# Another order of the second MLP product, projection operands ahead of the last norms, and loads a step apart, in a two-layer decoder trunk

## The chip, the cores and the metric

One core of one Trainium2 chip runs the kernel. The metric is device time in microseconds (us). Names of engines are those of the profile: PE is TensorE's matmuls, PEld its weight loads, DVE is VectorE, ACT is ScalarE, POOL is GpSimd, SP is SyncE, which issues most DMAs.

## What is computed

`x` is 1024 rows of 1024 float32 numbers. Two layers run one after the other: layer 0 mixes rows with causal pooling, layer 1 with a gated DeltaNet. Behind each mixer stand a norm, a dense MLP with a gated embedding, and a second norm.

```python
for i in range(2):
    mix = pool_mixer(x, ...) if i == 0 else gated_deltanet(x, ...)
    x = layer_norm(ALPHA * x + mix, ln_gain[i, 0], ln_bias[i, 0])
    ff = square(relu(x @ w1[i])) @ w2[i]              # 1024 -> 4096 -> 1024
    pe = sigmoid(x @ gate_w[i] + gate_b[i]) * (p[i] @ ple_proj[i])
    x = layer_norm(ALPHA * x + ff + pe, ln_gain[i, 1], ln_bias[i, 1])
```

The DeltaNet projects `x` onto queries, keys, values, a gate `z` and two narrow columns (`x @ w_in`), convolves over rows, runs a recurrence over eight chunks of 128 rows whose state `St` passes from chunk to chunk, norms each chunk's output, and multiplies by `w_out`.

## The kernel before

**Arithmetic.** Nearly every float32 product is three matmuls: each operand is split into a high part (a cast on ACT, L68) and a remainder (a subtraction on DVE, L69), and `mm3` (L71) adds high x high, high x low and low x high. So what PE can start on is mostly decided by when ACT and DVE have split an operand, and before that by when the DMA into a `raw` tile has landed. There are three `raw` slots (L40), two slots each for the `wh` and `wl` split results (L39) and six `tmp` slots.

**Order of work.** The program is written in one order, and a scheduler at build time settles the order on each engine from it by priorities; each engine then runs its list in that order. Where an instruction waits, all behind it on the same engine wait.

**Layer 0, start** (`layer0`, L567): `pp` is a list of 16 units that multiply `p` by `ple_proj` and store the result (`embed_unit`, L173: six matmuls, an ACT copy, a DMA issued from ACT). Four of them run first (L601), the others by a tuple of counts per step (L655).

**Gate and first product.** `gate` (L234) ends with operands for a seven-product (Winograd) scheme of the MLP's two products; the last, `t3`, is cut from `ra` at L303. In `mlp` (L306), `prep_a` (L332) makes operands of `w1` and `multiply_a` (L366) uses them, three steps behind.

**Second product** (L478 to L551): seven products P1, P2, P5, P6, P7, P4, P3 of eight groups `g` each. A group is 24 matmuls of 128x512 (four row tiles `tt`, two halves, three matmuls); `prep_b` prepares one group ahead. Rows of tiles 0 to 3 are finished when P4 ends, tiles 4 to 7 when P3 ends. In P3 the norms of tiles 0 to 3 run at `g` = 1 to 4. `finish` (L676) stores a row tile and transposes it for the projection (`transpose_split`, L128). In layer 0 the calls are held back by a list with a lag of four, so that tiles 0 to 3 are transposed among the last norms, and tiles 4 to 7 in the first units of the projection. The last two groups of P3 are done tile by tile (L549), each tile with its norm behind it. I call these 48 matmuls the tail; layer 1 has 96 of them.

**Projection** (`project`, L691): units of 16 or 24 matmuls; the first are `ba` half 0 (L928 loads it), `K` 0 half 0, `K` 1 half 0, `ba` half 1. Their `w_in` tiles are loaded one unit ahead.

**Recurrence** (`chain`, L970; loop at L1130): for each chunk `n` the products on the state, the output, `turn(n - 1)` (ACT scales the output at L1104, PE transposes it at L1109) and the per-chunk norm. At the end of chunk 5 the code loads all four pieces of the first half of `w_out` (L1157). `mix_out` (L1170) multiplies by it and serves as filler in chunk 7.

Of the kernel before, what the change touches and what calls it, by code (L numbers as in the profile page):

```python
# [32 lines left out]
def trunk(ctx: ExitStack, tc: tile.TileContext, io: dict):  # L33
# [43 lines left out]
    def load_wsm(src):  # L77
        raw = new_raw()
        nc.sync.dma_start(raw, src)
        wh = wsm.tile([P, 8, P], F32R, tag="wh", name=nm("wh"))  # L80
        wl = wsm.tile([P, 8, P], F32R, tag="wl", name=nm("wl"))
        split(wh, wl, raw.rearrange("p (k c) -> p k c", k=8))
        return wh, wl

# [67 lines left out]

    def load_w_half(wk, src, nh):
        for kk in range(4):
            raw = new_raw().rearrange("p (k c) -> p k c", k=2)
            nc.sync.dma_start(
                raw, src[kk * 256:(kk + 1) * 256, nh * 512:(nh + 1) * 512].rearrange("(k p) c -> p k c", p=P))
            split(wk[0][:, 2 * kk:2 * kk + 2, :], wk[1][:, 2 * kk:2 * kk + 2, :], raw)
# [75 lines left out]
    def gate(i, x, acc, wk, gb, early, pending):  # L234
# [68 lines left out]
        cut(t3, ra)  # L303
        return (b11h, b11l), (b21h, b21l), t2, t1, t3, t4, (b22h, b22l)

    def mlp(i, r1, acc, row, finish=None, lag=0, out=None):  # L306
# [18 lines left out]
        with tc.tile_pool(name=f"mlp{i}", bufs=5) as q:  # L325
# [180 lines left out]
            left = []  # L506

            def norm(t):
                layer_norm(acc(t), stats(t), g2, b2, True, None if out is None else out[t * P:(t + 1) * P, :])
                if finish:  # L510
                    left.append(lambda t=t: finish(t))
                if len(left) > lag:
                    left.pop(0)()

            seq = [(k, g) for k in (P1, P2, P5, P6, P7, P4, P3) for g in range(8)]
# [4 lines left out]
            for n in range(3):  # L520
                prep_a(*order[n])
            for n, o in enumerate(order):
# [8 lines left out]
            for n, (k, g) in enumerate(seq):  # L531
                if n % 2 == 0 and 4 + n // 2 < 16:
                    load_w2(4 + n // 2)
                if (k, g) == (P3, 0):
# [17 lines left out]
        return left  # L552
# [14 lines left out]
    def layer0(pool):  # L567
# [33 lines left out]
        for f in pp[0:4]:  # L601
            f()
        del pload[0:2], pp[0:4]
# [5 lines left out]
        for step in range(11):  # L609
# [45 lines left out]
            for _ in range((0, 2, 4, 2, 2, 2, 0)[min(step, 6)]):  # L655
# [14 lines left out]
        return gate(0, x1, acc, wk, gb, early, []), acc  # L670

    with tc.tile_pool(name="l0", bufs=4) as pool:
        r1, acc = layer0(pool)
# [6 lines left out]
    left = mlp(0, r1, acc, 1, finish, 4)  # L680
# [10 lines left out]
    def project(gd, pool, x2, left, heads, g, ex, ahead):  # L691
# [234 lines left out]
        w = {}  # L926

        def load_ba():  # L928
            raw = new_raw().rearrange("p (k c) -> p k c", k=8)
            nc.sync.dma_start(raw.rearrange("p k c -> p (k c)"), io["w_in"][32])  # L930
            wb = [h4(new_tmp(F32R, "wb")) for _ in range(2)]
            for z, w4 in enumerate(wb):
                r = raw[:, 4 * z:4 * z + 4, :]
                A.copy(w4[:, :, 0:64], r[:, :, 0:64])
                V.tensor_tensor(w4[:, :, 64:128], r[:, :, 64:128], w4[:, :, 0:64].bitcast(F32), ALU.subtract)
            return wb, None
# [33 lines left out]
    def chain(gd, heads, g, ex):  # L970
# [154 lines left out]
        def run(pool, stats):  # L1125
# [3 lines left out]
            pp = embed1(pool)  # L1129
            for n in range(8):  # L1130
# [8 lines left out]
                both(solve, n)  # L1139
                both(kq, n + 1)  # L1140
# [5 lines left out]
                both(output, n)  # L1146
                both(turn, n - 1)
# [4 lines left out]
                if n == 6:  # L1152
                    for t in range(8):
                        nc.sync.dma_start(acc(t), x2_d[t * P:(t + 1) * P, :])
                if n == 5:
                    wk = new_wk()
                    load_w_half(wk, io["w_out"], 0)  # L1157
                    acc = new_acc()
                    fill = [lambda t=t: mix_out(oT, wk, acc, stats, t, 0) for t in range(8)]
            for k, f in enumerate(fill):  # L1160
                if k == 2:
# [22 lines left out]
    with tc.tile_pool(name="gd", bufs=1) as gd:  # L1184
# [3 lines left out]
        with tc.tile_pool(name="gdp", bufs=1) as pool:  # L1188
            project(gd, pool, x2, left, heads, g, ex, [(64, load0), (65, prepare)])
# [4 lines left out]
    with tc.tile_pool(name="l1", bufs=4) as pool:  # L1194
# [12 lines left out]
        r1 = gate(1, x3, acc, wk, gb, [], left)  # L1207
    mlp(1, r1, acc, 3, out=io["out"])
# [62 lines left out]
```

## Time and profile before

| | us |
|---|---|
| median of 3 runs | 2176.24 (2175.05 to 2176.48) |
| the profiled execution | 2175.76 |
| its span | 2174.0 |
| PE busy | 2128.4 (98%) |
| DVE busy | 1527.0 (70%) |
| ACT busy | 1065.9 (49%) |

PE is busy nearly throughout, so the idle stretches of PE, one by one, are what can be read for time: a row of the timeline gives the start of a group of instructions, its length, engine, line, operation, and in brackets how long the engine was idle before it and what ended the wait. The granted clock is 1.00 at 2.4 GHz and 0.50 at 1.2 GHz.

### The profile page before, as it was taken

The numbers are of one execution on the slowest core, as the hardware profiler recorded it, in microseconds if no ns is written. First come the engines' busy times: TensorE is split into PE (matmuls) and PEld (weight loads), VectorE is DVE, ScalarE is ACT, GpSimd is POOL, SyncE is SP. The second block draws the span as 40 slices with busy tenths as digits, with TensorE's granted clock in tenths as the row PEclk, the third lists the DMA queues.
The fourth block names the chain that finished last, engine by engine and source line by source line (L and its number), as shares of the span: only waits on it lengthen the run. The fifth ranks groups of instructions, "written<-read, shape, count | busy, mean of one in ns | idle before, by whom it ended". The sixth has DMA issues, their size and how long they took to land.

```text
span 2174.0 us, 27706 instructions
## 1 busy us (share of the span) xinstructions
PE 2128.4 (98%) x10322; PEld 1780.0 (82%) x10322; DVE 1527.0 (70%) x2569; ACT 1065.9 (49%) x1822; POOL 25.2 (1%) x85
## 2 busy tenths in 40 slices
PE   7999999999999989999999999999999999999998
PEld 7977888887888868888888998888788888788886
DVE  7996666667765676879976677588666666677458
ACT  6434555553333446644456666453355555433334
POOL 0000000000000000000001000000000000000000
PEclk9999999999999999999999999999999999999999
DMA  8324444469333241341233545312344445943223
GB/s 303 111 83 146 151 151 143 152 225 334 100 116 97 97 163 49 100 124 49 92 131 109 139 127 177 95 68 83 117 150 159 151 147 178 331 155 116 97 96 126
DMA packets 156700, 300.98 MB, mean 138 GB/s; under 512 B 39891, under 2 KB 53587, under 8 KB 156245
## 3 DMA queue, kind: packets, MB, share of 16 engines
q1 hardware_dynamic: 151956, 290.82, 40.4%
q10 hardware_dynamic: 4608, 8.39, 1.0%
q8 instruction: 81, 1.33, 0.3%
q14 instruction: 55, 0.44, 0.1%
HBM read 208.99 MB, written 90.18 MB: 138 GB/s over the span
## 4 chain that ended last, share of the span: by engine, by line
PE 91%; DVE 4%; DMA 2%; ACT 2%; issue 1%; SPq 0%; ACTq 0%; DVEq 0%
PE ps L75 27%; PE ps L74 27%; PE ps L73 27%; PE ps L134 1%; PE ps L801 1%; DMA raw<-in_w 1%; PE ps L775 1%; PE ps L1057 1%; PE ps L1021 1%; PE ps L1079 1%; PE ps L1045 0%; PE ps L1050 0%; PE ps L1066 0%; DMA raw<-in_gate 0%; PE ps L1014 0%
## 5 line engine op out<-in xcount | busy, mean ns | idle before, releaser
L73 PE MATMUL ps<-rh,lh 128*128 128x512 f32 x896 | 349.2, 391 | 4.3 <-ACT rh L68 3.7
L74 PE MATMUL ps<-rl,lh 128*128 128x512 f32 x896 | 349.0, 390 | 0.3 <-DVE rl L69 0.3
L75 PE MATMUL ps<-rh,ll 128*128 128x512 f32 x896 | 349.0, 390 | 0.0
L68 ACT CAST lh<-raw 128x1024 fp32r<-128x1024 f32 x112 | 118.2, 1055 | 342.3 <-PE ps L74 325.7
L69 DVE TENSOR_TENSOR rl<-w,rh 128x1024 fp32r<-128x1024 f32 x110 | 134.6, 1224 | 185.5 <-issue 165.4
L73 PE MATMUL ps<-xh,wo 128*128 128x512 f32 x512 | 200.1, 391 | 3.0 <-ACT wo L68 1.6
L73 PE MATMUL ps<-xh,wh 128*128 128x512 f32 x512 | 202.7, 396 | 0.0
L73 PEld LDWEIGHTS ps<-rh,lh 128*128 128x128 f32 x896 | 168.5, 188 | 40.6 <-ACT rh L68 4.6
L75 PE MATMUL ps<-xh,wl 128*128 128x512 f32 x512 | 200.0, 391 | 1.1 <-DVE wl L69 1.1
L75 PE MATMUL ps<-xh,wo 128*128 128x512 f32 x512 | 199.8, 390 | 0.0
L74 PE MATMUL ps<-xl,wo 128*128 128x512 f32 x512 | 199.7, 390 | 0.0
L74 PE MATMUL ps<-xl,wh 128*128 128x512 f32 x512 | 199.4, 389 | 0.0
L74 PEld LDWEIGHTS ps<-rl,lh 128*128 128x128 f32 x896 | 168.6, 188 | 35.9 <-DVE rl L69 1.0
L75 PEld LDWEIGHTS ps<-rh,ll 128*128 128x128 f32 x896 | 168.5, 188 | 35.0 <-DVE ll L69 0.3
L69 DVE TENSOR_TENSOR wo<-raw,wo 128x512 fp32r<-128x512 f32 x192 | 132.1, 688 | 52.2 <-ACT wo L68 52.2
L68 ACT CAST wo<-raw 128x512 fp32r<-128x512 f32 x192 | 119.3, 621 | 99.3 <-PE ps L75 70.3
L324 DVE TENSOR_TENSOR c<-ps,c 128x512 f32<-128x512 f32 x96 | 66.4, 692 | 135.1 <-PE ps L75 72.6
L73 PE MATMUL ps<-xt,wo 128*128 128x512 f32 x384 | 149.8, 390 | 2.1 <-ACT wo L68 2.1
L74 PE MATMUL ps<-xt,wo 128*128 128x512 f32 x384 | 149.6, 390 | 0.0
L75 PE MATMUL ps<-xt,wo 128*128 128x512 f32 x384 | 149.0, 389 | 0.0
L69 DVE TENSOR_TENSOR ll<-raw,lh 128x1024 fp32r<-128x1024 f32 x112 | 136.7, 1220 | 6.7 <-ACT lh L68 6.4
L68 ACT CAST rh<-w 128x1024 fp32r<-128x1024 f32 x110 | 115.1, 1049 | 5.3 <-DMA h_d<-c 2.7
(304 smaller groups left out, 4164.8 us busy)
## 6 DMA issues: line engine op xcount, KB each, us to landing
raw<-h_d SPq DMA_DIRECT2D x112, 512.0 KB, 3.3
raw<-in_w SPq DMA_DIRECT2D x64, 512.0 KB, 3.6
w<-in_w SPq DMA_DIRECT2D x32, 1024.0 KB, 6.6
h_d<-c SPq DMA_DIRECT2D x64, 512.0 KB, 2.8
raw<-in_w_in SPq DMA_DIRECT2D x41, 512.0 KB, 3.6
h_d<-hs SPq DMA_DIRECT2D x32, 512.0 KB, 3.6
pp_d<-tmp ACTq DMA_DIRECT2D x32, 256.0 KB, 3.8
raw<-in_gate SPq DMA_DIRECT2D x16, 512.0 KB, 5.3
```

Source lines behind the costliest of these rows:

```text
L68: A.copy(hi, src)
L69: V.tensor_tensor(lo, src, hi.bitcast(F32), ALU.subtract)
L73: T.matmul(ps, lh, rh, start=first, stop=False, skip_group_check=more)
L74: T.matmul(ps, lh, rl, start=False, stop=False, skip_group_check=more)
L75: T.matmul(ps, ll, rh, start=False, stop=last, skip_group_check=more)
L134: T.transpose(pss[q][:, j, :], y[:, k * P:(k + 1) * P], ident)
L324: add = lambda o, a, b: V.tensor_tensor(o, a, b, ALU.add)
L775: T.transpose(ps[:, j, :], chunk(tiles, half * 4 + j, h), ident)
L801: T.matmul(ps[:, j, :], kc, kc, start=True, stop=True)
L1021: T.matmul(pq[:, j, :], hc("K", n, h), hc("Q", n, h), start=True, stop=True)
L1057: T.matmul(pv[:, j, :], d["X"][:, h, :], d["c"][:, 2 + gi, j], start=True, stop=True)
L1079: T.matmul(po[:, j, :], d["dt"][gi][:, j, :], d["c"][:, 4 + gi, j], start=True, stop=True)
```

## The change

1. Layer 0 starts with two `pp` units and not four; the two others run at step 0.
2. `gate` hands back the cut of `t3`, and `mlp` calls it after its first three `prep_a`.
3. The second product runs P1, P5, P6, P7, P4, P2, P3. Tiles 0 to 3 are finished after the fifth of them; their norms run in the sixth (P2) at `g` = 1, 3, 5, 7, and their `finish` in P3 at `g` = 0 to 3. The operand of P4 is made in P4 and no longer in P6, and `w2` comes in the order in which the products want it.
4. `load_ba` moves out of `project`. The operands of the first two units (`ba`, `K` 0) are loaded and split at the head of the tail, `K` 1 ahead of its last row tile; the split tiles of `K` 0 take two of the three `raw` slots, since both `wsm` slots are in use.
5. The four pieces of `w_out` are fetched at chunk 4 (end), 5 (middle), 5 (end) and 6 (start), each split one such point later (`w_step`). `turn(7)` moves one `mix_out` back.

```diff
-        cut(t3, ra)
-        return (b11h, b11l), (b21h, b21l), t2, t1, t3, t4, (b22h, b22l)
+        return [(b11h, b11l), (b21h, b21l), t2, t1, t3, t4, (b22h, b22l)], lambda: cut(t3, ra)
...
-                f, c, e, b = n // 4 % 2, n // 8, n // 2 % 2, n % 2
+                (f, c), e, b = ((0, 0), (0, 1), (1, 1), (1, 0))[n // 4], n // 2 % 2, n % 2
...
-                    sub(b21, b21, b11)
...
                 elif k == P4:
-                    r = b21
+                    sub(b11, b21, b11)
+                    r = b11
...
-            seq = [(k, g) for k in (P1, P2, P5, P6, P7, P4, P3) for g in range(8)]
+            seq = [(k, g) for k in (P1, P5, P6, P7, P4, P2, P3) for g in range(8)]
...
             for n in range(3):
                 prep_a(*order[n])
+            cut_t3()
...
-                if k == P3 and 0 < g < 4:
-                    norm(g - 1)
-                if k == P3 and g == 4:
-                    norm(3)
+                if k == P2 and g % 2:
+                    norm(g // 2)
+                if k == P3 and g < 4 and finish:
+                    finish(g)
...
+                    if last and ahead and tt in (0, 3):
+                        for f in ahead[tt]:
+                            f()
...
-        for f in pp[0:4]:
+        for f in pp[0:2]:
...
-            for _ in range((0, 2, 4, 2, 2, 2, 0)[min(step, 6)]):
+            for _ in range((2, 2, 4, 2, 2, 2, 0)[min(step, 6)]):
...
+    ahead = {0: [lambda: load_first(("ba", 0), None), lambda: load_first(("K", 0), rawp)],
+             3: [lambda: load_first(("K", 1), None)]}
...
+                kk = {(4, 2): 0, (5, 0): 1, (5, 2): 2, (6, 0): 3, (6, 1): 4}.get((n, z))
...
+                    split_w(wk, kk - 1, raw.pop(kk - 1))
+                if kk < 4:
+                    raw[kk] = fetch_w(io["w_out"], 0, kk)
...
-                    wk = new_wk()
-                    load_w_half(wk, io["w_out"], 0)
```

What the scheduler makes of it is seen at three places. The first is DVE at the head of the projection. Before, the remainders of `ba` (`wb`) stand between the steps of the last norms (L108 to L121 is one norm):

```order
L69 TENSOR_TENSOR wl_820_6127<-raw_818_6124,wh_819_6126 128x1024
L113 RECIPROCAL lnsm_206_1634<-lnsm_206_1634 128x1
L108 SCALAR_TENSOR_TENSOR acc_15_154<-acc_15_154,lnsm_206_1634,gb_745_5662 128x1024
L118 SCALAR_TENSOR_TENSOR lnsm_206_1634<-lnsm_206_1634 128x1
L109 TENSOR_SCALAR lnsm_206_1634<-lnsm_206_1634 128x1
L935 TENSOR_TENSOR wb_816_6118<-raw_815_6116,wb_816_6118 128x4x64
```

After, both `wb` and the remainder of `K` 0 (`wl_798`) stand ahead of the first take of the tail (L502):

```order
L91 TENSOR_TENSOR wb_794_5985<-raw_793_5983,wb_794_5985 128x4x64
L91 TENSOR_TENSOR wb_795_5986<-raw_793_5983,wb_795_5986 128x4x64
L69 TENSOR_TENSOR rl_792_5978<-w2_558_4378,rh_791_5977 128x1024
L69 TENSOR_TENSOR ll_790_5976<-raw_788_5973,lh_789_5975 128x1024
L69 TENSOR_TENSOR wl_798_5994<-raw_796_5991,wh_797_5993 128x1024
L502 SCALAR_TENSOR_TENSOR acc_15_154,lnsm_206_1630<-ps_539_4244,acc_15_154 128x512
```

So the operands of the first two units moved from among the last steps of the norms to ahead of all four. The second place is ACT in chunk 6. Before, two `w_out` casts (`wkh`), with their waits for DMAs, stand ahead of the eight scalings that PE's transposes wait for (L1104):

```order
L68 CAST wkh_1508_10958<-raw_1512_10968 128x1024
L1058 COPY ctr_1487_10802<-ps_1532_11052 128x512
L68 CAST wkh_1508_10958<-raw_1513_10972 128x1024
L68 CAST phl_1523_11019<-praw_1522_11018 128x256
L1008 COPY wt_1530_11044<-ps_1529_11035 64x512
L68 CAST oh_1556_11242<-oT_1354_9982 128x1024
L68 CAST oh_1561_11284<-oT_1354_9982 128x1024
L1104 ACTIVATE ctr_1448_10570<-ctr_1448_10570,f_1506_10935 128x128 x8
```

After:

```order
L1068 COPY ctr_1490_10806<-ps_1531_11046 128x512
L68 CAST oh_1556_11242<-oT_1354_9982 128x1024
L1114 ACTIVATE ctr_1448_10570<-ctr_1448_10570,f_1510_10943 128x128 x4
L68 CAST wkh_1472_10740<-raw_1532_11054 128x1024
L1114 ACTIVATE ctr_1448_10570<-ctr_1448_10570,f_1510_10943 128x128 x4
L68 CAST oh_1561_11284<-oT_1354_9982 128x1024
```

One cast and one `oh` moved out from ahead of the scalings, and the last piece of `w_out` now stands in the middle of them. The third place is ACT in the first 25 us. Before, four copies (L179) with their DMA issues (L180) stand between the two halves of `zt`, of which the last two, the second half of `zt`, `bias` and the next `wh` are:

```order
L179 COPY tmp_21_182<-ps_20_175 128x512
L179 COPY tmp_23_192<-ps_22_185 128x512
L180 DMA pp_d_78<-tmp_21_182 128x512
L180 DMA pp_d_78<-tmp_23_192 128x512
L68 CAST zt_11_131<-ps_26_211 128x512
L648 CAST bias_227<-pbr_126 128x1024
L68 CAST wh_28_233<-raw_27_231 128x1024
```

After, two of the four stand behind `wh`:

```order
L68 CAST zt_11_131<-ps_22_191 128x512
L661 CAST bias_207<-pbr_126 128x1024
L68 CAST wh_24_213<-raw_23_211 128x1024
L194 COPY tmp_28_228<-ps_27_221 128x512
L194 COPY tmp_30_238<-ps_29_231 128x512
```

## Rows read from the trace of the kernel before

**Rows 1.** The page, busy time of each engine, its share of the span, instructions

```profile
PE 2128.4 (98%) x10322; PEld 1780.0 (82%) x10322; DVE 1527.0 (70%) x2569; ACT 1065.9 (49%) x1822; POOL 25.2 (1%) x85
```

**Rows 2.** Timeline of PE, groups behind an idle stretch (idle and releaser in brackets)

```profile
22.05 0.58 PE L73 MATMUL ps<-zt,b0h 128*128 128x256 f32 x1 [2.35 <-ACT zt L68]
...
806.11 0.76 PE L953 MATMUL ps<-xh,wb 128*128 128x512 f32 x1 [9.19 <-DVE lnsm L112]
...
1337.10 1.50 PE L1109 MATMUL ps<-identr,ctr 128*128 128x128 f32 x5 [3.37 <-ACT ctr L1104]
...
1553.44 0.66 PE L73 MATMUL ps<-xt,wo 128*128 128x512 f32 x1 [1.05 <-ACT wo L68]
...
2147.75 0.50 PE L73 MATMUL ps<-rh,lh 128*128 128x512 f32 x1 [0.56 <-ACT lh L68]
```

**Rows 3.** Windows: from:to, length, busy us of PE, PEld, DVE, ACT, POOL; clock, DMA

```profile
1318.40:1323.40 5.00, 5.00 (x46) 5.00 (x46) 3.78 (x8) 4.86 (x15) 0.00 (x0) 1.00 0.59 186
21.00:28.00 7.00, 5.43 (x22) 4.85 (x23) 5.48 (x8) 3.42 (x4) 0.00 (x0) 0.51 0.85 267
...
761.00:767.00 6.00, 6.00 (x29) 4.95 (x28) 5.93 (x11) 3.81 (x6) 0.00 (x0) 1.00 0.82 310
...
799.00:810.00 11.00, 3.90 (x10) 3.16 (x11) 10.03 (x22) 5.89 (x10) 0.00 (x0) 0.53 0.57 201
1338.60:1345.40 6.80, 6.80 (x35) 5.66 (x35) 4.26 (x10) 2.57 (x9) 0.00 (x0) 0.50 0.42 159
1553.60:1557.00 3.40, 3.40 (x9) 2.61 (x10) 3.40 (x7) 1.24 (x2) 0.00 (x0) 0.50 1.02 393
```

**Rows 4.** Timeline of PE in the first projection unit, at either clock

```profile
806.67 0.63 PE L954 MATMUL ps<-xl,wb 128*128 128x512 f32 x1
...
809.23 0.53 PE L954 MATMUL ps<-xl,wb 128*128 128x512 f32 x1
809.60 0.40 PE L953 MATMUL ps<-xh,wb 128*128 128x512 f32 x1
...
811.19 0.39 PE L954 MATMUL ps<-xl,wb 128*128 128x512 f32 x1
```

**Rows 5.** Timeline of ACT in the first 25 us

```profile
19.87 1.07 ACT L179 COPY tmp<-ps 128x512 f32<-128x512 f32 x2 [0.68 <-ACT tmp L179]
...
21.41 0.59 ACT L68 CAST zt<-ps 128x512 fp32r<-128x512 f32 x1 [0.47 <-ACT tmp L179]
```

**Rows 6.** Timeline of ACT ahead of layer 1's MLP

```profile
1547.96 2.01 ACT L68 CAST xt<-ra 128x1024 fp32r<-128x1024 f32 x2 [3.73 <-PE ps L74]
```

**Rows 7.** Timelines of DVE and ACT from the tail to the projection

```profile
783.11 1.22 DVE L69 TENSOR_TENSOR ll<-raw,lh 128x1024 fp32r<-128x1024 f32 x1
...
785.63 0.68 DVE L487 SCALAR_TENSOR_TENSOR acc<-ps,acc 128x512 f32<-128x512 f32 x1
...
786.67 0.69 DVE L139 TENSOR_TENSOR xl<-ps,xh 128x512 fp32r<-128x512 f32 x1 [0.35 <-ACT xh L137]
...
788.79 1.28 DVE L108 SCALAR_TENSOR_TENSOR acc<-acc,lnsm,gb 128x1024 f32<-128x1024 f32 x1 [1.31 <-ACT junk L106]
...
806.01 0.16 DVE L113 RECIPROCAL lnsm<-lnsm 128x1 f32<-128x1 f32 x1
...
807.40 0.42 DVE L935 TENSOR_TENSOR wb<-raw,wb 128x256 fp32r<-128x256 f32 x1
...
804.02 0.69 ACT L934 CAST wb<-raw 128x256 fp32r<-128x256 f32 x2
```

**Rows 8.** Timelines of SP, ACT and DVE in chunk 6 of the recurrence

```profile
1323.77 1.76 SPq L156 DMA_DIRECT2D raw<-in_w_out  x2
...
1332.77 1.05 ACT L68 CAST wkh<-raw 128x1024 fp32r<-128x1024 f32 x1 [3.24 <-DMA raw<-in_w_out]
...
1336.65 2.45 ACT L1104 ACTIVATE ctr<-ctr,f 128x128 f32<-128x128 f32 x8
...
1333.85 1.22 DVE L69 TENSOR_TENSOR wkl<-raw,wkh 128x1024 fp32r<-128x1024 f32 x1 [3.27 <-ACT wkh L68]
```

More of the change, by code (lines that the diff above doesn't have):

```diff
@@ L75, in mm3, with load_wsm, load_ba @@
         T.matmul(ps, ll, rh, start=False, stop=last, skip_group_check=more)
-    def load_wsm(src):
+    def load_wsm(src, pool=None):
         raw = new_raw()
         nc.sync.dma_start(raw, src)
-        wh = wsm.tile([P, 8, P], F32R, tag="wh", name=nm("wh"))
-        wl = wsm.tile([P, 8, P], F32R, tag="wl", name=nm("wl"))
+        wh, wl = ((pool or wsm).tile([P, 8, P], F32R, tag="raw" if pool else s, name=nm(s)) for s in ("wh", "wl"))
         split(wh, wl, raw.rearrange("p (k c) -> p k c", k=8))
         return wh, wl
+    def load_ba():
+        raw = new_raw().rearrange("p (k c) -> p k c", k=8)
+        nc.sync.dma_start(raw.rearrange("p k c -> p (k c)"), io["w_in"][32])
+        wb = [h4(new_tmp(F32R, "wb")) for _ in range(2)]
+        for z, w4 in enumerate(wb):
+            r = raw[:, 4 * z:4 * z + 4, :]
+            A.copy(w4[:, :, 0:64], r[:, :, 0:64])
+            V.tensor_tensor(w4[:, :, 64:128], r[:, :, 64:128], w4[:, :, 0:64].bitcast(F32), ALU.subtract)
+        return wb, None
     def load_bc(pool, row):
@@ L151, in new_wk, with fetch_w, split_w @@
         return k8("wkh"), k8("wkl")
+    def fetch_w(src, nh, kk):
+        raw = new_raw().rearrange("p (k c) -> p k c", k=2)
+        nc.sync.dma_start(
+            raw, src[kk * 256:(kk + 1) * 256, nh * 512:(nh + 1) * 512].rearrange("(k p) c -> p k c", p=P))
+        return raw
+    def split_w(wk, kk, raw):
+        split(wk[0][:, 2 * kk:2 * kk + 2, :], wk[1][:, 2 * kk:2 * kk + 2, :], raw)
     def load_w_half(wk, src, nh):
         for kk in range(4):
[L155 to L158, printed above, removed]
+            split_w(wk, kk, fetch_w(src, nh, kk))
     def cols(nh):
@@ L302, in gate, with mlp @@
         t3 = new_t()
-        cut(t3, ra)
-        return (b11h, b11l), (b21h, b21l), t2, t1, t3, t4, (b22h, b22l)
-    def mlp(i, r1, acc, row, finish=None, lag=0, out=None):
+        return [(b11h, b11l), (b21h, b21l), t2, t1, t3, t4, (b22h, b22l)], lambda: cut(t3, ra)
+    def mlp(i, r1, cut_t3, acc, row, finish=None, ahead=None, out=None):
         P1, P2, P6, P5, P7, P4, P3 = range(7)
@@ L551, in mlp @@
                         norm(4 + tt)
-        return left
+        return [lambda t=t: finish(t) for t in range(4, 8)]
     x2_d = dram.tile([S, D], F32, name="x2_d")
@@ L678, in finish, with load_first @@
         transpose_split(acc(t), x2, t)
-    left = mlp(0, r1, acc, 1, finish, 4)
+    first = {}
+    def load_first(key, pool):
+        first[key] = load_ba() if key[0] == "ba" else load_wsm(io["w_in"][8 + key[1]], pool)
+    ahead = {0: [lambda: load_first(("ba", 0), None), lambda: load_first(("K", 0), rawp)],
+             3: [lambda: load_first(("K", 1), None)]}
+    left = mlp(0, r1, cut_t3, acc, 1, finish, ahead)
     def sm(pool, s, dt=F32):
@@ L689, in chunk, with project @@
         return tiles[n // 4][:, h, (n % 4) * P:(n % 4 + 1) * P]
-    def project(gd, pool, x2, left, heads, g, ex, ahead):
+    def project(gd, pool, x2, left, first, heads, g, ex, ahead):
         xh, xl = x2
@@ L925, in project @@
             at(u, f)
[L926 to L936, printed above, removed]
+        w = dict(first)
         def weights(k):
@@ L1129, in run, with w_step @@
             pp = embed1(pool)
+            wk, raw = None, {}
+            def w_step(n, z):
+                nonlocal wk
+                kk = {(4, 2): 0, (5, 0): 1, (5, 2): 2, (6, 0): 3, (6, 1): 4}.get((n, z))
+                if kk is None:
+                    return
+                if kk == 0:
+                    wk = new_wk()
+                else:
+                    split_w(wk, kk - 1, raw.pop(kk - 1))
+                if kk < 4:
+                    raw[kk] = fetch_w(io["w_out"], 0, kk)
             for n in range(8):
@@ L1188, in trunk @@
         with tc.tile_pool(name="gdp", bufs=1) as pool:
-            project(gd, pool, x2, left, heads, g, ex, [(64, load0), (65, prepare)])
+            project(gd, pool, x2, left, first, heads, g, ex, [(64, load0), (65, prepare)])
         with tc.tile_pool(name="gdc", bufs=1) as pool:
@@ L1206, in trunk @@
         load_w_half(wk, io["gate"][1], 0)
-        r1 = gate(1, x3, acc, wk, gb, [], left)
-    mlp(1, r1, acc, 3, out=io["out"])
+        r1, cut_t3 = gate(1, x3, acc, wk, gb, [], left)
+    mlp(1, r1, cut_t3, acc, 3, out=io["out"])
 def _layout(i):
```

18 lines of the change are left out of this document (8 added, 10 removed).

## The prediction

> **What bounds the kernel now.** I began with the busy times: PE works 2128.4 of 2174.0 us [rows 1]. The change removes and adds no matmul, so only PE's idle stretches and its stretches at half clock can go. The second view is PE's timeline, read for the brackets that give an idle stretch and its releaser [rows 2]: the reader is to see that the large ones are few, 9.19 us at the head of the projection, 3.37 in chunk 6 of the recurrence, 2.35 at the start, 1.05 at an MLP's start (0.79 of the same kind stand just ahead of it, and layer 0 has the same pair), 0.56 near the end. The third is the table of windows [rows 3]: the granted clock is 0.50 to 0.53 in four places, each behind or within such a stretch. What half clock costs is read in one product that runs through the change [rows 4]: six matmuls between 806.67 and 809.23 start 0.427 us apart, seven from 809.60 to 811.19 start 0.227 apart. So a matmul of 128x512 loses 0.2 us, and a stretch at half clock loses about 47% of its length. I sum against the profiled execution, 2175.76 us (span 2174.0 and 1.8 around it), which is 0.5 under the median of 2176.24.
>
> **Start of layer 0.** PE idles 2.35 us for the second half of `zt`, which ACT casts at 21.41 behind two `pp` copies from 19.87 on with their DMA issues [rows 5]. These two copies now stand behind `bias` and `wh`. The cast can come up to 21.41 - 19.87 = 1.5 us earlier. PE loses the cover of 12 matmuls there and waits for `pwt` instead, earlier; the 12 come back as fill. I take -1.5. Bounds: -3 if the half clock of 21 to 28 goes too (at most 3.3 us by the 47%), +1 if the copies, now among step 0's norm, hold it up.
>
> **Start of both MLPs.** Two casts of `t3` take 2.01 us of ACT [rows 6] ahead of an operand for which PE then idles [rows 2]. In the new order these casts still stand ahead of the operand on ACT; on DVE, though, an add and a subtraction for the next operands have moved ahead of the remainders of `t3`, and PE has products that need `t3` to run meanwhile. Of the pair of waits (1.84 us a layer) I take 1.1 away in each layer; in layer 1 also a little of the half clock of 1553.6 to 1557.0, whose 3.4 us cost 1.6 [rows 3]: -1.1 and -1.3. Bounds: 0 and 0, or -1.8 and -3.4.
>
> **Second product.** The counts of splits, subtractions, norms and loads stay; so does the pattern of accumulators (P2's first matmuls wait for takes of P4 where P5's waited for those of P2). What moves are four norms from P3 to P2, every second group, and eight transposes a group into P3. Before, both lay together: from 761 to 767 DVE was busy 5.93 of 6.00 us, and PE still 6.00 of 6.00 at full clock [rows 3]. Spread out they cost nothing; if DVE were late by a whole norm a group, that is the slow rival below. One new wait: the tail now has no transposes to fill in. The last group's left operand needs slots that the group before the tail frees, so its cast and remainder (1.22 on DVE [rows 7], about as much on ACT) lie beside only six matmuls, 6 x 0.227 = 1.4 us, though PE's list has the next tile's matmuls in between. I take +0.5 (0 to 1.1). In layer 1 the norms of tiles 0 to 3 leave the stretch ahead of the 0.56 us wait [rows 2], a wait for a load that had no `raw` slot, because each norm takes one: -0.8 with what stands beside it (0 to -0.9). The last norm and the store behind the last matmul are unchanged.
>
> **Head of the projection.** Before, PE waits from 796.9 to 806.11 for `wb`, whose cast ACT makes at 804.02 and whose second remainder DVE makes at 807.40, among the last norms [rows 7]. DVE is the busy one: 10.03 of 11.00 us from 799 to 810 [rows 3]. The change puts `wb` and `K` 0 ahead of the tail's takes. What goes is 9.19, and 8 x 0.2 = 1.7 for the half clock behind it: 10.9. What is late next? From the start of the tail, PE has 48 + 16 matmuls (tail, `ba`) = 14.5 us, then a transpose of tile 4, then 24 (`K` 0) = 5.4, so it asks for tiles 5 and 6 at about 21, then `K` 1, so for tile 7 at about 28. DVE has until then: 1.1 waiting for the last cast, two splits of 1.22, then per norm two passes of 1.28, a take of 0.68 and some seven small steps like the 0.16 one [rows 7], 4.4 in all, and between the norms of tiles 5 and 6 the remainder of `K` 1 (1.22). Three norms are done at 1.1 + 2.4 + 13.2 + 1.2 = 18, four at 23, plus waits on ACT of up to 3. So tiles 5 and 6 come just in time, tile 7 with 2 us to spare. DVE fits because the eight remainders of `finish` (0.69 each, 5.5 us) have left the tail. Behind the `K` 1 remainder, which waits on PE for its slot until the last but one group's use ends (about 9.5), stand the norms of tiles 6 and 7; on SP, `cmats` waits for the single `raw` slot left by `K` 0, and behind it `hr` and the `w_in` loads of later units, wanted only after six units. I take -10.5, with bounds -6 (DVE 3 us late and a new half clock) and -12.5 (also the smaller gaps before and behind).
>
> **Chunk 6.** ACT waits 3.24 us for the last piece of `w_out`, DVE 3.27 behind it; both stand ahead of the scalings from 1336.65 that PE waits 3.37 us for [rows 2, 8]. The two last pieces were issued together at 1323.77 [rows 8], so the last landed nine us later. A step apart, three of the four are split before that point; the fourth now stands between the fourth and fifth scaling. Its load needs the slot that the third piece's remainder frees, by my estimate at 1328 to 1330 (before, DVE was through with that one by 1333.85 - 3.27 = 1330.6). The two loads together took nine us, so one takes about 4.5, and the cast of 1.05 ends at 1333.5 to 1335.5, while PE is done with chunk 6 at 1333.7 and first has four transposes of the first half to do. I leave 0.6 us of wait. Gone: 2.8, and the half clock from 1338.6 to 1345.4, 47% of 6.8 = 3.2 [rows 3], and about 0.3 beside. I take -6.3. Bounds: -1 (fourth piece as late as before, clock falls again), -8.5 (all that the stretch loses). The price is that `ple` and the loads for the recurrence (`dt` of chunks 6 and 7) share `raw` slots with the pieces: `dt` of 6 is issued later, behind the `ple` load. No row sizes its slack; each us by which it comes too late costs one, and the bound of -1 holds 5 of them.
>
> **Sum.** -1.5 - 1.1 - 1.3 + 0.5 - 0.8 - 10.5 - 6.3 = -21.0: 2154.8 in the profiled execution, about 2155 as a median. All low ends together (3 + 1.8 + 3.4 + 0.9 + 12.5 + 8.5 = 30.1) give 2146; all high ends (+1 + 1.1 - 6 - 1 = -4.9) 2171.
>
> **A rule against it.** From 1318.4 to 1323.4 PE begins with 16 transposes, and the clock stays 1.00 [rows 3]. The Trainium skill, "TensorE: Matmul & The Clock Gate", section "Part 4: PE-mode transpose", says that transposes don't count as busy PE in the way matmuls do. By that rule the 16 transposes now side by side between `K` 0 and `K` 1 could bring half clock there; at the price of the stretch of 1553.6 the sum would be -19.4. The row speaks against it; I keep -21.0.
>
> **The rivals.** *DVE stays the bound at the projection's head.* The wait for `wb` becomes one for tiles 5 and 6, because each norm also waits on ACT's pass and its root. For it: DVE's 10.03 of 11.00. Against: the 5.5 us that leave. With 3 us of wait and 1.7 of half clock the projection gives -5.8, in all 2159.5. Chance 0.2.
>
> *The clock falls anyway.* Waits of about 1 us are left at the start, in chunk 6 and at layer 1's MLP, and one of 1.05 was enough at 1553.44 [rows 2, 3], though layer 0's like pair brought none. Then the start gives 0, chunk 6 gives 3.2 less, and layer 1's MLP costs what it did: 1.5 + 3.2 + 1.3 and one new stretch of 1.6, so 2155 + 7.6 = 2162.5. Chance 0.12.
>
> *Slower: norms ahead of operands in P2.* DVE's list puts parts of a norm between the remainders of a group. If the next group's operands wait for them, each of eight norms (four a layer) costs up to the two passes and both splits, 2 x 1.28 + 2 x 1.22 = 5.0, 40 us in all, so 2195. It makes the kernel slower by over 0.2% from (21 + 4.4) / 8 = 3.2 us a norm. Against it: the same norms beside more work cost PE nothing from 761 to 767. Chance 0.04.
>
> *The scheduler leaves the gaps.* The `w_out` piece among the scalings is as late as before and the casts of `t3` stay where they are: 5.3 and 2.4 less, 2163. Chance 0.1.
>
> **How the numbers follow.** The forecast, -15 to -27, has 0.51; the rivals 0.2, 0.12, 0.1 and 0.04; 0.03 is left for a gain within 0.2% or an unseen fault. The first three rivals still end faster. A measurement of this kernel can tell 0.2%, 4.4 us, from no change. Faster: 0.51 + 0.2 + 0.12 + 0.1, less 0.02 for two rivals at once, 0.91; same 0.05; slower 0.04. The range goes from 2147, short of all low ends, to 2168, which takes in each rival but the slow one, and two of them partly together.
>
> **What would show it.** At the head of the projection, `ba`'s matmuls should follow the tail without a bracket, and the next bracket, if any, should stand before the transposes of tiles 5 and 6 with DVE as releaser. In chunk 6 the bracket of 3.37 should be under 1.5, with ACT's fourth `w_out` cast just before it and clock 1.00 behind. The groups of P2 should show no bracket. The forecast is wrong if PE waits behind P2's norms, if `dt` of chunk 6 shows as a releaser, or if half clock shows at new places for over 10 us.

## The result, and the profile after

The changed kernel takes 2150.11 us, the median of four runs (2147.30 to 2153.37); the kernel before takes 2175.82 over four runs beside it (2175.05 to 2176.48). The ratio is 0.9882, with a 95% interval from 0.9865 to 0.9900: 25.7 us less by the medians, against a forecast of 21 and a range of 2147 to 2168. The profiled execution of after is the slowest of its four, 2153.37 (span 2151.6), so the two traces differ by 22.4 only.

The first view is the page's busy times of after; it answers to [rows 1].

```profile
PE 2121.5 (99%) x10322; PEld 1774.7 (82%) x10322; DVE 1528.8 (71%) x2569; ACT 1064.2 (49%) x1822; POOL 24.8 (1%) x85
```

The instructions are the same in number on every engine. PE is busy 6.9 us less for the same 10322 matmuls, which is in the main time at half clock that has gone, and the other 15.5 of the span's 22.4 are idle stretches of PE.

The second view is PE's timeline of after at the places of [rows 2] and ahead of the second products; the bracket gives the idle time before a group and its releaser.

```profile
22.35 0.39 PE L73 MATMUL ps<-pwt,wh 128*128 128x256 f32 x1 [0.88 <-ACT wh L68]
...
51.64 0.38 PE L639 MATMUL ps<-zt,band 128*128 128x256 f32 x1 [0.56 <-DVE zt L69]
...
60.44 0.39 PE L639 MATMUL ps<-zt,band 128*128 128x256 f32 x1 [0.76 <-DVE zt L69]
...
489.68 1.20 PE L73 MATMUL ps<-rh,lh 128*128 128x512 f32 x4 [1.85 <-ACT rh L68]
...
795.08 0.39 PE L963 MATMUL ps<-xh,wb 128*128 128x512 f32 x1
...
805.08 1.91 PE L143 MATMUL ps<-identr,acc 128*128 128x128 f32 x16
...
814.19 0.51 PE L963 MATMUL ps<-xh,wb 128*128 128x512 f32 x1 [0.87 <-ACT xh L146]
...
1343.75 0.50 PE L75 MATMUL ps<-wkh,ol 128*128 128x512 f32 x1 [0.31 <-DVE ol L69]
...
1531.75 0.50 PE L73 MATMUL ps<-xt,wo 128*128 128x512 f32 x1 [0.68 <-ACT c L400]
...
1842.48 1.35 PE L73 MATMUL ps<-rh,lh 128*128 128x512 f32 x4 [1.85 <-ACT rh L68]
```

The bracket of 9.19 at the head of the projection has no successor: from the tail through `ba`, `K` 0 and the sixteen transposes of tiles 5 and 6 PE waits for nothing, and the 0.87 at 814.19 stood in before too, at the same point of the work. That of 3.37 in chunk 6 has gone, and that of 2.35 at the start has become 0.88, as forecast for `pwt`; in its place two others have come, of 0.56 and 0.76 at 51.64 and 60.44, where before waits for nothing.

The third view is the table of windows of after (from:to, length, busy us of PE, PEld, DVE, ACT, POOL; granted clock, DMA), for the same work as [rows 3] and for both second products.

```profile
484.00:494.00 10.00, 7.89 (x29) 5.76 (x28) 8.64 (x10) 4.72 (x6) 0.00 (x0) 0.88 1.02 354
708.00:751.00 43.00, 43.00 (x195) 35.74 (x194) 32.20 (x53) 20.14 (x25) 0.00 (x0) 1.00 0.40 147
783.80:799.00 15.20, 15.20 (x69) 12.24 (x68) 13.50 (x28) 7.12 (x12) 0.14 (x2) 1.00 0.28 87
799.00:812.00 13.00, 13.00 (x70) 11.10 (x69) 12.89 (x28) 11.71 (x19) 1.14 (x2) 1.00 0.50 179
1310.00:1330.00 20.00, 20.00 (x174) 18.46 (x173) 16.38 (x53) 16.24 (x52) 0.00 (x0) 1.00 0.51 165
1838.00:1848.00 10.00, 8.05 (x28) 5.79 (x27) 8.03 (x9) 4.09 (x4) 0.00 (x0) 0.83 1.00 343
```

The norms among P2's groups (708 to 751) leave PE busy 43.00 of 43. At the projection's head DVE is busy 12.89 of 13.00 us and PE still 13.00. The clock is 1.00 at the projection and in chunk 6, where it was 0.53 and 0.50. Half clock is left at the start of both second products (0.88 and 0.83 in their windows), in layer 1 at a place where the profile of before had none.

Set beside each other, stage by stage, each stage running from one row of PE behind a bracket to the next (plain differences of start times in the two profiled executions, in us; the rows start at 478.81, 826.90, 1186.00, 1363.78, 1512.15 and 1852.02 in before and at 476.64, 814.19, 1173.29, 1343.75, 1492.35 and 1829.44 in after):

| stage | before | after | difference | forecast |
|---|---|---|---|---|
| start and start of layer 0's MLP | 478.81 | 476.64 | -2.2 | -2.6 |
| second product of layer 0 and head of the projection | 348.09 | 337.55 | -10.5 | -10.0 |
| rest of the projection | 359.10 | 359.10 | 0.0 | 0 |
| recurrence, with chunk 6 | 177.78 | 170.46 | -7.3 | -6.3 |
| layer 1's gate | 148.37 | 148.60 | +0.2 | 0 |
| layer 1's MLP, start and first product | 339.87 | 337.09 | -2.8 | -1.3 |
| second product of layer 1, end | 321.98 | 322.16 | +0.2 | -0.8 |

The terms sum to -22.4. What is missing to the 25.7 of the medians is that this execution was after's slowest; the last section comes back to it.

### The profile page after: what moved, and what is told of

Its sections match the earlier page's. It is cut to its first block, busy times and chain, and to the rows that moved or that the text cites. A ratio compares the mean times of both kernels' runs of the same rounds, so it can differ in the third digit from the quotient of the medians.

```text
span 2151.6 us, 27702 instructions
## 1 busy us (share of the span) xinstructions
PE 2121.5 (99%) x10322; PEld 1774.7 (82%) x10322; DVE 1528.8 (71%) x2569; ACT 1064.2 (49%) x1822; POOL 24.8 (1%) x85
## 4 chain that ended last, share of the span: by engine, by line
PE 92%; DVE 4%; DMA 2%; ACT 2%; issue 1%; SPq 0%; DVEq 0%; ACTq 0%
PE ps L75 28%; PE ps L74 28%; PE ps L73 28%; DMA raw<-in_gate 1%; PE ps L143 1%; PE ps L1067 1%; PE ps L1031 1%; PE ps L821 1%; PE ps L1089 1%; PE ps L795 1%; DMA raw<-in_xTt 1%; PE ps L1060 1%; PE ps L1055 1%; PE ps L1076 1%; PE ps L1024 0%
```

## The experiments

Ten kernels were run, one of them after itself and the others each a change to it. Where their stages are compared, the stage "layer 0" is from the first matmul behind the 1.85 us wait of the second product (489.68 in after) to the 0.87 us wait in the projection (814.19): 324.51 us in after, 335.06 in before. Half clock behind the 1.85 us wait costs it 1.2 to 1.6 us in some executions (e4 has 324.13 and after 324.51 with it, e3 322.89 without, in code that is the same there); after, before, e1, e4, e5 and e9 have it, e2, e3, e6, e7 and e10 haven't.

**After itself, for the spread.** The kernel is unchanged.

> The changed kernel itself, for its spread (its four runs lie between 2147.3 and 2153.4, those of before within 1.5 us). Theory: what differs between executions is where the clock falls for 3.4 us, 1.6 us each; then this profile shows the same brackets within 0.1 us but half clock at other places than the start of the second products of both layers. Rival: a load lands late in some executions; then the brackets themselves differ by 1 us or more.

It took 2149.98 (2148.70 to 2151.10), ratio 0.9886 [0.9869, 0.9902], with layer 0 at 324.13. The theory held in half. The brackets differ from after's by at most 0.65 us (the first is 1.02 at 13.82 for 0.40 at 13.65), and half clock moves: layer 1's second product has none, where after's trace has 3.4 us of it, and 3.4 us stand from 15.4 on, where after has none. At layer 0's second product, though, both traces have it. e1, e2 and e3 ran on the same chip and are compared with this one.

**Without the operands ahead of the norms.**

```diff
-    left = mlp(0, r1, cut_t3, acc, 1, finish, ahead)
+    left = mlp(0, r1, cut_t3, acc, 1, finish)
```

> The changed kernel with one part taken back: the operands of ba, K 0 and K 1 are loaded and split in the projection again, no longer at the tail of the MLP. My theory (DVE and ACT are free enough once the transposes have left the tail, and what counted was that wb stood behind the norms in their lists): the bracket before the first ba matmul comes back, but smaller than 9.19 us, since eight remainders of 0.69 have left DVE there; 4 to 8 us with the half clock, so some 2154 to 2158 where the changed kernel gives 2150. Rival (the earlier norms alone freed the operands, the calls ahead do nothing): within 1 us of the changed kernel. Rival (the whole gain is the calls ahead): all of 10.5 us comes back, 2160 to 2161.

It took 2163.71 (2162.87 to 2164.28), ratio 0.9951 [0.9936, 0.9965]: 13.7 us over e4, as much as the whole gain at this place and more; of the times expected, the rival's in which the calls ahead are all (2160 to 2161) is the nearest. My theory fell in one half: the 5.5 us of `finish` remainders that leave the tail should have made the wait smaller than 9.19 by themselves. Its other half, that `wb` stands behind the norms in the lists, is what the rows show. PE's, ACT's and DVE's timelines of this kernel:

```profile
804.22 0.76 PE L963 MATMUL ps<-xh,wb 128*128 128x512 f32 x1 [10.79 <-DVE lnsm L122]
...
797.45 1.28 ACT L748 ACT_TABLE_LOAD   x1 [2.19 <-DMA hr<-in_hrow]
...
799.01 1.28 ACT L120 ACT_TABLE_LOAD   x1
...
801.55 0.70 ACT L90 CAST wb<-raw 128x256 fp32r<-128x256 f32 x2
...
800.54 0.16 DVE L122 RECIPROCAL lnsm<-lnsm 128x1 f32<-128x1 f32 x1 [1.56 <-ACT lnsm L120]
```

This trace reaches the second product 4.0 us sooner than before's, so the times are counted from the matmul behind the 1.85 us wait, at 487.85 here and at 491.84 in before. PE is done with the tail 305.6 us behind it (305.1 in before) and has `wb` at 316.4 (314.3): `wb` is ready 2.1 us later than in before, and the wait is longer by 1.6. The new order by itself makes layer 0's stage 336.97, 1.9 over before. What holds `wb` back is ACT's list: ahead of its cast stand a wait of 2.19 for the load of `hr`, the table load for `Exp`, the one for the norms behind it, and the last norm. DVE is not the one that is late there: it idles 1.56 us itself, for the root on ACT.

**The same, with the Exp later in ACT's list.** Its input is made to depend on a value that comes later (plus zero times it); the result is the same.

```diff
 (besides the edit of the experiment above)
-            A.activation(ea, hr[:, 0, :], AF.Exp)
+            V.scalar_tensor_tensor(ea, e, 0.0, hr[:, 0, :], ALU.mult, ALU.add)
+            A.activation(ea, ea, AF.Exp)
```

> The kernel of e1 (operands not ahead), in which Exp of the a_log row now takes its input from a copy that depends on the gate logits, so that its two table loads and its wait for the hr load can't stand among the last norms (the copy adds 0 times a finite number, so values stay). In e1, ACT lost 5.0 us from 795.3 to 800.3 to that wait and the two table loads, ahead of the cast of wb, and PE idled 10.8. Theory (place in ACT's list, not load on DVE, makes wb late): the bracket before ba's first matmul falls by 2.5 to 5 us, the kernel by 3 to 5 us to about 2159 to 2161. Rival (DVE's norms hold wb): the bracket stays over 9.5 us and the time within 1 us of e1's 2163.7.

It took 2160.84 (2160.44 to 2161.30), ratio 0.9943 [0.9928, 0.9958], as expected; it ran on another chip than e1, and the intervals of the two ratios overlap. The traces tell them apart: the bracket shrinks by 3.2, and layer 0's stage from 336.97 to 334.28. PE's and ACT's timelines of this kernel:

```profile
801.85 0.76 PE L964 MATMUL ps<-xh,wb 128*128 128x512 f32 x1 [7.63 <-DVE lnsm L121]
...
798.49 0.20 ACT L120 ACTIVATE lnsm<-lnsm 128x1 f32<-128x1 f32 x1 [2.44 <-DVE lnsm L118]
798.62 1.15 ACT L115 ACTIVATE junk<-acc,lnsm 128x1024 bf16<-128x1024 f32 x1
...
799.76 0.69 ACT L90 CAST wb<-raw 128x256 fp32r<-128x256 f32 x2
```

So some 3 us of the wait were the `Exp` with its wait and its two table loads. The other 7.63 are the norms: the cast still stands behind the pass of the last one, for which ACT itself waits 2.44 on a small step of DVE.

**Only `ba` ahead.** `K` 0 and `K` 1 are left to the projection, as before.

```diff
-    ahead = {0: [lambda: load_first(("ba", 0), None), lambda: load_first(("K", 0), rawp)],
-             3: [lambda: load_first(("K", 1), None)]}
+    ahead = {0: [lambda: load_first(("ba", 0), None)]}
```

> The changed kernel with only ba's operands called ahead, K 0 and K 1 in the projection again. Theory (each operand waits where its cast and remainder stand in the lists): ba follows the tail without a wait, and PE then waits for K 0, whose remainder now stands behind the norms of tiles 4 to 6 in DVE's list: 3 to 6 us and half clock for some of it, 2153 to 2157. Rival (ba's wait was all; K 0 comes in time by itself): within 1 us of the changed kernel.

It took 2149.72 (2149.00 to 2152.29), ratio 0.9891 [0.9877, 0.9906]: no different from after, so my theory that `K` 0 has to come along fell. DVE's and PE's timelines of this kernel:

```profile
796.07 2.35 DVE L69 TENSOR_TENSOR wl<-raw,wh 128x1024 fp32r<-128x1024 f32 x2
...
810.99 0.49 PE L962 MATMUL ps<-xh,wb 128*128 128x512 f32 x1 [0.86 <-ACT xh L146]
```

Both remainders are made from 796.07 on, while PE has `ba` to do, and PE has no bracket before the usual one at 810.99. So with the new order in place, the whole gain of the calls ahead is the place of `wb` ahead of the last norms.

**`K` 1 called at the head of the tail too.**

```diff
-             3: [lambda: load_first(("K", 1), None)]}
+    ahead = {0: [..., lambda: load_first(("K", 1), None)]}
```

> The changed kernel with the operands of K 1 called at the head of the tail as well. Theory (what stands in DVE's list behind an instruction that waits is held too): the remainder of K 1 waits for a slot that the last but one group frees near the tail's end, so the takes and norms of tiles 4 to 6 start about 4 us later if it stands ahead of them, and PE waits 2 to 4 us at the transposes of tiles 5 and 6: 2152 to 2155. Rival (the scheduler puts it where its slot is free, so the call's place is nothing): within 1 us of the changed kernel, 2149 to 2151.

It took 2151.26 (2150.28 to 2151.68), ratio 0.9898 [0.9883, 0.9913], with layer 0 at 322.99, equal to e10's 323.19. The rival held: the call is earlier in the text, but the remainder of `K` 1 stands in practically the same place of DVE's list, 8.0 us behind the first take of the tail here (785.51) and 8.4 in after (787.54). DVE's timelines, of this kernel and of after:

```profile
793.55 1.22 DVE L69 TENSOR_TENSOR wl<-raw,wh 128x1024 fp32r<-128x1024 f32 x1
...
795.89 1.23 DVE L69 TENSOR_TENSOR wl<-raw,wh 128x1024 fp32r<-128x1024 f32 x1
```

**The order of the seven products as before, the operands still ahead.**

```diff
-            seq = [(k, g) for k in (P1, P5, P6, P7, P4, P2, P3) for g in range(8)]
+            seq = [(k, g) for k in (P1, P2, P5, P6, P7, P4, P3) for g in range(8)]
-                if k == P2 and g % 2:
-                    norm(g // 2)
-                if k == P3 and g < 4 and finish:
-                    finish(g)
+                if k == P3 and 0 < g <= 4:
+                    norm(g - 1)
                     if last:
                         norm(4 + tt)
+                        if finish:
+                            finish(tt)
 (and the order of the w2 loads, the load of the norms' gains and the operand of P4 as before)
```

> The changed kernel with the second product back in the order P1, P2, P5, P6, P7, P4, P3, norms of tiles 0 to 3 in P3, their transposes in the tail, w2 and P4's operand as before; the calls ahead of the tail stay. My theory (DVE is the bound at the head of the projection, and fits only because 5.5 us of remainders left the tail): PE's wait moves from ba to the transposes of tiles 4 to 6, with DVE as releaser, 4 to 7 us with the half clock, so 2154 to 2157, and layer 1's wait of 0.56 us near the end returns. Rival (the order of the products is worth nothing, the calls ahead are all): within 1 us of the changed kernel but for the 0.6 in layer 1.

It took 2154.31 (2153.00 to 2155.89), ratio 0.9908 [0.9893, 0.9923]: 4.3 over e4; the time is as expected, the way to it only in part. PE's timeline of this kernel:

```profile
791.76 0.50 PE L963 MATMUL ps<-xh,wb 128*128 128x512 f32 x1 [0.93 <-ACT xh L146]
...
795.02 0.66 PE L143 MATMUL ps<-identr,acc 128*128 128x128 f32 x4 [1.15 <-DVE acc L502]
...
2125.14 0.50 PE L73 MATMUL ps<-rh,lh 128*128 128x512 f32 x1 [0.58 <-ACT lh L68]
```

With the transposes back in the tail PE waits twice at the head of the projection, for a tile's `xh` and for a take of DVE: 2.1 us at full clock, where 4 to 7 with half clock, for DVE alone, were expected. Layer 0's stage is 2.9 us longer (325.83 against e3's 322.89, both at full clock), and the 0.56 us wait of layer 1 [rows 2] is back as 0.58. Together with e1 this says that the order and the operands ahead belong together: the order alone gains nothing in layer 0, the operands alone most of it (9.2 us of the stage, 1.2 to 1.6 of them for half clock that this trace lacks), and the last 3 us need both.

**`w_out`'s pieces together, as before.**

```diff
-                kk = {(4, 2): 0, (5, 0): 1, (5, 2): 2, (6, 0): 3, (6, 1): 4}.get((n, z))
+                kk = None
 (and load_w_half in chunk 5 and the place of turn(7) as before)
```

> The changed kernel with the four pieces of w_out loaded together at the end of chunk 5 again and turn(7) at its old place. My theory: PE's wait of 3.37 us in chunk 6 comes back whole, with ACT's scaling as releaser, and half clock behind it: 6 to 7.5 us more than the changed kernel, so about 2156 to 2158. Rival (half clock follows its own course, the wait alone counts): 3 to 4 us more.

It took 2156.14 (2155.12 to 2157.91), ratio 0.9917 [0.9902, 0.9932]: 6.2 over e4, as expected. PE's timeline of this kernel, and its window behind the bracket:

```profile
1321.35 1.64 PE L1119 MATMUL ps<-identr,ctr 128*128 128x128 f32 x5 [2.84 <-ACT ctr L1114]
...
1320.70:1330.90 10.20, 9.55 (x44) 7.76 (x45) 7.09 (x19) 5.79 (x20) 0.00 (x0) 0.50 0.38 137
```

The wait is back with 10.2 us at half clock, and the recurrence takes 178.01 us, as in before (177.78), against 170.46 in after. The edit takes back the spread loads and the place of `turn(7)` together; what each is worth is not shown.

**`t3` cut in the gate again, ahead of the first operands.**

```diff
-        return [(b11h, b11l), (b21h, b21l), t2, t1, t3, t4, (b22h, b22l)], lambda: cut(t3, ra)
+        cut(t3, ra)
+        return [(b11h, b11l), (b21h, b21l), t2, t1, t3, t4, (b22h, b22l)], lambda: None
```

> The changed kernel with t3 cut in gate again, in both layers. Theory: a pair of waits of about 0.8 and 1.05 us comes back ahead of both first products where the changed kernel has one of 0.7 to 0.8, so 1.0 us a layer, and the half clock of 3.4 us at layer 1's first product may come back with them: 2 to 3.6 us, 2152 to 2153.6. Rival (the casts stand where they stood, so nothing moves): within 0.5 us.

It took 2153.53 (2150.63 to 2153.84), ratio 0.9906 [0.9892, 0.9921], 2.3 over e6 on the same chip, with one of its four runs as low as e6's. PE's timeline of this kernel:

```profile
176.59 0.50 PE L73 MATMUL ps<-xh,wo 128*128 128x512 f32 x1 [1.01 <-ACT wo L68]
...
178.37 0.80 PE L73 MATMUL ps<-xt,wo 128*128 128x512 f32 x1 [1.05 <-ACT wo L68]
...
1532.57 0.50 PE L73 MATMUL ps<-xt,wo 128*128 128x512 f32 x1 [1.05 <-ACT wo L68]
```

The pair of waits is back in both layers. Here half clock follows in both (178.2 to 181.6 and 1533.3 to 1536.7, 0.50); in before the same pair brought it in layer 1 only. Layer 1's MLP, from the row at 1491.31 to that at 1831.23, takes 339.92 us again (339.87 in before, 337.09 in after).

**The start as before.**

```diff
-        for f in pp[0:2]:
+        for f in pp[0:4]:
-        del pload[0:2], pp[0:2]
+        del pload[0:2], pp[0:4]
-            for _ in range((2, 2, 4, 2, 2, 2, 0)[min(step, 6)]):
+            for _ in range((0, 2, 4, 2, 2, 2, 0)[min(step, 6)]):
```

> The changed kernel with the start of layer 0 as before (four pp units first, none at step 0). Theory: the wait of 2.35 us for the second half of zt comes back, with the half clock behind it, where the profiles of the changed kernel's start show two waits of 0.5 to 1.0 near 12.5 and 13.7, and one of up to 0.9 near 22: 1.5 to 3 us, 2151.5 to 2153. Rival (the start only moves the same wait, DVE decides up to 140 us): within 1 us.

It took 2151.83 (2149.29 to 2153.32), ratio 0.9895 [0.9879, 0.9912], 2.1 over e10 on the same chip, but their ranges overlap by most of their length. The bracket of 2.34 is back at 21.92, with 0.51 of the clock from 23.9 to 27.4; that the wait returns is shown, what it costs is not settled. The two traces differ by 4.3, but e9's has half clock at both second products and e10's at neither.

```profile
21.92 0.38 PE L73 MATMUL ps<-zt,b0h 128*128 128x256 f32 x1 [2.34 <-ACT zt L68]
```

**A version that removes the next wait.** After waits 1.85 us at the start of each second product, ahead of the second group. ACT's timeline of after shows why:

```profile
482.42 1.06 ACT L68 CAST lh<-raw 128x1024 fp32r<-128x1024 f32 x1 [1.46 <-PE ps L75]
...
487.63 1.04 ACT L68 CAST lh<-raw 128x1024 fp32r<-128x1024 f32 x1 [2.97 <-PE ps L74]
488.59 1.04 ACT L68 CAST rh<-w 128x1024 fp32r<-128x1024 f32 x1
```

The second group's left operand is cast at 482.42. The cast of the third group's left operand waits 2.97 for the first group's matmuls to free its slot, and the second group's right operand queues behind it. In this kernel the second group's right operand takes four `tmp` slots, which are free by then.

```diff
+                elif k == P1 and g == 1:
+                    lh, ll = new_op("lh", "wh"), new_op("ll", "wl")
+                    rh, rl = [new_tmp(F32R, "rh") for _ in range(2)], [new_tmp(F32R, "rl") for _ in range(2)]
+                    split(lh, ll, l)
+                    for j in range(2):
+                        split(rh[j], rl[j], r[:, j])
 (and the matmuls take rh as two halves)
```

> The changed kernel with one addition: the right operand of the second product's second group takes four tmp slots and no longer two slots of the pool that the first product's results hold until their stores have landed. In the changed kernel PE idles 1.85 us ahead of that group in both layers, for the cast of rh, which stands in ACT's list behind the cast of the third group's lh, which waits for PE. Theory: both waits go, and with them the half clock that followed them in most profiles: 3.7 us, up to 6.9, so 2143 to 2146.5. Rival (the load of that group's other operand, or the third group's slots, is late next): a wait of 1 to 2 us comes one group later and the gain stays under 1.5 us.

It took 2144.57 (2142.98 to 2145.03), ratio 0.9866 [0.9850, 0.9883], as expected: 6.7 under e6 on the same chip (2151.26), with ranges that don't meet. It beats both kernels. Its windows at the start of the two second products:

```profile
484.00:494.00 10.00, 10.00 (x45) 8.28 (x45) 8.84 (x10) 5.06 (x5) 0.00 (x0) 1.00 0.98 344
1836.00:1846.00 10.00, 10.00 (x46) 8.29 (x45) 7.87 (x8) 4.69 (x5) 0.00 (x0) 1.00 0.97 330
```

PE is busy 10.00 of 10 in both, at full clock, where after had 7.89 at 0.88 and 8.05 at 0.83. Against e6, which has both waits without half clock, layer 0 takes 2.8 us less from the MLP's start to the projection (333.19 against 336.02) and layer 1 2.7 less from the MLP's start to the end (318.15 against 320.85); Of the first, 2.7 arise between 487 and 492, where e6 has the brackets of 1.85 and 0.25. 1.1 more lie ahead of both, in the spread of the start. Where half clock follows the wait, there are up to 1.6 us more to gain at each place.

## Why the prediction held, and where not

**Head of the projection, -10.5 with +0.5 beside it: the size held (-10.5 for both together), the reason behind it only in part.** The forecast said that DVE is the bound, and that the eight remainders leaving the tail are what lets it fit. e1 took away the operands and kept the lighter DVE: `wb` came 2.1 us later in the stage than in before, and not sooner. e5 and e10 show what made the wait: ACT's two casts for `wb` stood behind a load, two table loads and a norm, and it is enough to put `ba` ahead of them. DVE's 10.03 of 11.00 us [rows 3] was read as a bound of `wb`; in after DVE is busy 12.89 of 13.00 with PE at 13.00 of 13. A releaser named "DVE lnsm" in the bracket of 9.19 [rows 2] only says which instruction ended last, and the row of ACT's cast at 804.02 [rows 7] should have been followed back to what stood ahead of it on ACT. That the forecast came out at the measured size is no proof of its reason: whatever had held `wb`, the bracket and the half clock behind it were there to take. The lighter DVE counts only for what is late next: with the remainders back in the tail (e2) the stage lost 2.9 us. The +0.5 for the last group's left operand did not come; there is no bracket in the tail. The part on what is late next held: tile 6's last pass on DVE ends at 804.33, and PE begins the sixteen transposes of tiles 5 and 6 at 805.08. DVE's timeline of after:

```profile
803.06 1.27 DVE L130 SCALAR_TENSOR_TENSOR acc<-acc,lnsm,gb 128x1024 f32<-128x1024 f32 x1
```

0.8 us is left there, or 1.6 if tile 6's eight are the later ones (from 805.95), so the rival in which DVE makes PE wait for tiles 5 and 6 was near, and did not come.

**Chunk 6, -6.3: held, -7.3.** The 0.6 us that I left for the fourth piece were not needed. SP's and ACT's timelines of after:

```profile
1316.20 0.37 SPq L164 DMA_DIRECT2D raw<-in_w_out  x1
...
1318.40 1.28 ACT L1114 ACTIVATE ctr<-ctr,f 128x128 f32<-128x128 f32 x4 [0.50 <-DVE f L1107]
1319.74 1.05 ACT L68 CAST wkh<-raw 128x1024 fp32r<-128x1024 f32 x1
1320.69 1.28 ACT L1114 ACTIVATE ctr<-ctr,f 128x128 f32<-128x128 f32 x4
```

The fourth piece is issued at 1316.20 and its cast, between the fourth and fifth scaling, waits for nothing at 1319.74: it had landed within 3.5 us, against my 4.5. The price that I had set against it, `dt` of chunks 6 and 7 coming late, shows in no bracket.

**Layer 1's MLP, -1.3: mis-sized, -2.8.** The term took 1.1 of the waits and "a little" of the half clock. The waits fell to 0.68, and the half clock of 1553.6 to 1557.0 went whole, near the bound of -3.4. e7 takes back the edit, and pair, half clock and 2.8 us return together; in one of its four runs (2150.63) they seem not to cost so much.

**End, -0.8: mis-sized, +0.2 in this trace.** The 0.56 us wait went, as said. But after's trace has half clock from 1843.4 to 1846.8 behind the 1.85 us wait, where the trace of before has the same wait and none; this belongs to the execution and not to the change, for e4 runs the same kernel without it and takes 320.83 us from the row at 1828.47 to the end, 1.2 less than before and not 0.2 more. The waits of 1.85 stood in before, and the forecast rightly gave them to neither side, but it left them out of its list of large waits, and in counting four places at half clock it missed a fifth, which stood behind the first of them. PE's timeline and the window there, of before:

```profile
491.84 1.90 PE L73 MATMUL ps<-rh,lh 128*128 128x512 f32 x4 [1.85 <-ACT rh L68]
...
488.00:498.00 10.00, 8.15 (x29) 6.15 (x28) 5.26 (x6) 4.09 (x4) 0.00 (x0) 0.83 1.03 358
```

**Start, -1.5 and -1.1: held in sum, -2.2.** The first matmul of layer 0's MLP parts the two terms. PE's timeline there, of before and of after:

```profile
176.28 0.39 PE L73 MATMUL ps<-xh,wo 128*128 128x512 f32 x1
...
175.24 0.39 PE L73 MATMUL ps<-xh,wo 128*128 128x512 f32 x1
```

From there to the row that ends the first stage of the table before takes 302.53 us and after 301.40, 1.1 less as forecast for `t3`. The nine other traces with the new cut take 301.2 to 301.6, e7 with the old one 304.19. The start gave 1.0 in this pair, of 1.5. PE idles 3.6 us from 8 to 30 in before and 2.0 in after, as forecast; but from 30 to that matmul it idles 0.9 in before and 2.2 in after, for the waits at 51.64, 60.44 and 139.84, so most of it came back, and the half clock that went from 21 to 28 is most of what is left of the gain. The size is not settled: the matmul stands at 172.6 to 175.2 in the ten traces with the new start, and at 175.7 (e9) and 176.3 (before) in those with the old.

**The rivals.** The slow one, norms ahead of operands in P2, is not seen: 43.00 of 43.00 us. That the scheduler leaves the gaps is not seen either. That the clock falls anyway came in part, at places where the forecast did not look: at layer 1's second product in after, and near 15 us in six of the other traces. The case against the forecast by a rule, from the Trainium skill, "TensorE: Matmul & The Clock Gate", section "Part 4: PE-mode transpose" (transposes don't count as matmuls do): the half clock that it could have brought did not come, with clock 1.00 from 799 to 812, where 16 transposes stand side by side among matmuls (805.08). Before has 16 side by side as well, at 817.76, so they were not new with the change; eight more traces have them, and the clock stays 1.00 there in all ten.

## What to carry to other kernels

When a wait names a norm's small step on the busiest engine, follow the late operand back on every engine that makes it: here a cast of 0.7 us stood behind a load, two table loads and a norm on an engine that was busy half the time, and one load, two casts and two remainders put ahead of them were worth more than taking 5.5 us off the busy engine. Compare such times from an instruction that both traces share, not from the start of the program. Fetch loads that pass through the same slots a step apart, and look for the waits that begin a stage: the 1.85 us at each second product was a cast queued behind one that waited for a slot, and other free slots took it away for 5.5 us more. A short wait of PE should be priced with the half clock that may follow it, as a range: with a stretch of 3.4 us at half clock behind it (up to 1.6 us more) and without.

## What the runs showed of the hardware

The same wait brings half clock in one execution and not in the next. The 1.85 us wait ahead of layer 0's second product is followed by 3.4 us at half clock in the traces of before, after, e1, e4, e5 and e9, and by none in those of e2, e3, e6, e7 and e10; in layer 1 it is so in after, e1, e2 and e9 alone. PE's work up to there is the same in most of them, so a single pair of traces can be off by up to 1.6 us at each such place; the four runs of after lie 6 us apart, those of before 1.4. What decides it no run here tells. Nor does half clock always cost time: of the ten traces with the new start six have 3.4 us of it near 15 us, and they reach layer 0's MLP at 172.6 to 174.9, the four without at 173.4 to 175.2.

A table load on ACT takes 1.28 us in every row here. The Trainium skill, "ScalarE: Activation LUTs", section "Table sets: the hidden batching unit", counts about 2.7 us for each; here the row decides, for the `Exp` behind the load at 801.72 in after begins at 803.01. Two of them with a late load were worth some 3 us together.
